# Two projections of a two-block transformer: one product over 512 columns in place of two over 256

## The chip, the cores and the metric

The kernel runs on one core of one Trainium2 chip. The metric is the device time of one execution in microseconds (us), the median of the runs shown. Five engines work beside each other and meet only at semaphores: PE (TensorE) multiplies matrices, PEld is its loading of weights, DVE (VectorE) and ACT (ScalarE) do the elementwise work, POOL (GpSimd) a few memsets, and SP (SyncE) issues the DMAs that bring the weights in.

## What is computed

256 tokens of width 2048 pass through two blocks in float32. The first block is an attention mixer followed by a feed-forward part, the second is another attention mixer with its own projections. What the change touches are the products of two large projections:

```python
def conv_geglu_ffn(h, w_up, conv_w, conv_b, w_down):
    u = h @ w_up                                   # 2048 -> 2 * 5632
    up = jnp.pad(u, ((0, 0), (1, 1), (0, 0)))
    u = conv_b + sum(up[:, t:t + S] * conv_w[t] for t in range(3))
    gate, val = jnp.split(u, 2, axis=-1)
    return (jax.nn.gelu(gate, approximate=True) * val) @ w_down
...
h = _rmsnorm(x, norm_g[l])                         # second block
proj = h @ w_in[l]
(qa, kca, vca, ksa, vsa, kwa, vwa, za, ga, qb, kb, vb, zb) = jnp.split(proj, offsets, axis=-1)
```

## The kernel before

**Number format.** TensorE multiplies a reduced float32 format here, so every float32 operand is held as a sum of two such numbers, a high and a low part. A product x·w is taken as high·high + high·low + low·high. An activation tile `h` (or `g`) is 128 x 512: columns 0 to 255 are the high parts of the 256 tokens, columns 256 to 511 their low parts. A weight tile of 128 x 128 exists as `hi` and as `lo`.

**A unit of product.** `mm3` (lines 326 to 332) handles one weight tile with three matmuls of 256 columns into the same 256 columns of a PSUM bank: `hi` by the high half (L329), `hi` by the low half (L330), `lo` by the high half (L331). `job_t` makes 128-column output tiles of these: for two output tiles at a time (`per=2`) it runs through the 16 weight tiles of one, then of the other, so that a pair takes 32 units. Both tiles of the pair share one PSUM bank of 512 float32 columns, 256 each. When the last unit is in, it queues the eviction `evac(i, ps)`. 3712 units in the program go through `mm3`.

**Weight stream.** All weights come in pieces of 128 x 1024 float32 (eight weight tiles) through 12 buffers `raw`. Per chunk of four weight tiles ACT makes `hi` (L290, a cast) and DVE makes `lo` (L291, raw minus hi), into six buffers of each; `execute` keeps four chunks ahead of the unit at hand. A `raw` buffer is fetched anew as soon as its last reader is done.

**Evictions.** In the feed-forward part `up` gives each pair (one gate tile, one value tile) to `glu`, which reads the bank directly: for each half an ACT activation (L1208, centre tap and bias) and two DVE operations (L1209, L1211, the side taps), then the gelu, a product (L1216) and the split into high and low parts (L503, L504). In the second block `tiles` hands the bank to a rotary embedding (`rope`) or to a gate (`ev_z`), which read it directly too. Between the units of the feed-forward part, every 20 of them, a batch of another product is woven in that runs on DVE alone (`ada_dve`, L456, straight from `raw`).

**Order.** The program is written as a list of units with side work that is advanced once every four units (`tick`); a scheduler then puts each engine's instructions into a fixed order. An engine executes its own list in that order and waits where an operand isn't there. Stages in time: up-projection of tiles 4 to 21 (about 545 to 752 us), half of the down-projection (to 879), up-projection of tiles 22 to 43 (to 1132), the other half (to 1286), second input projection and its attention heads (about 1300 to 1620), output projection.

Of the kernel before, what the change touches and what calls it, by code (L numbers as in the profile page):

```python
# [22 lines left out]
T = 256  # L23
D = 2048
KT = 16
EPS = 1e-6
NEG = -1e30
DFF = 5632
# [106 lines left out]
class Body:  # L135
# [8 lines left out]
        self.uid = 0  # L144
        self.active, self.waiting, self.now, self.last = [], [], 0, -99

    # ------------------------------------------------------------ tiles
    def nm(self, s):
        self.uid += 1
        return f"{s}_{self.uid}"  # L150
# [27 lines left out]
        o, w = CST[n]  # L178
        return self.ct[:, o + a:o + (w if b is None else b)]

    # ------------------------------------------------------------ cooperative side work
    def spawn(self, gen, group="", paced=False):
        (self.waiting if paced else self.active).append([gen, group, 0])

# [35 lines left out]
            v = get()  # L220
        return v

    # ------------------------------------------------------------ weight stream
    def flatten(self, prog):
        self.flat, self.plan, self.chunks = [], [], []
        self.uses = {}
        run = -1
        for u in prog:
            if u.kind == "c":
                self.flat.append(("c", u.fn, 0, 0, 0))  # L230
                continue
            if u.kind == "p":
                while len(self.plan) % PB:
                    self.plan.append(self.plan[-1])
                continue
            left, off = u.n, 0
            while left:
                pos = len(self.plan)
                room = PB - pos % PB
                n = min(left, room) if u.split else left  # L240
                assert n <= room
                for i in range(n):
                    self.plan.append((u.mat, u.kt, u.c0 + 128 * (off + i)))
                p = pos // PB
                if u.kind == "w":
                    c = self.chunks[-1] if self.chunks else None
                    if c is None or c[1] != pos or pos % PB == 0 or pos + n - c[0] > self.CHUNK:
                        self.chunks.append([pos, pos])
                        self.uses[p] = self.uses.get(p, 0) + 1
                    self.chunks[-1][1] = pos + n  # L250
                    fn = (lambda a, f=u.fn, o=off: f(a, o)) if u.split else u.fn
                    self.flat.append(("w", fn, pos, n, len(self.chunks) - 1))
                else:
                    self.uses[p] = self.uses.get(p, 0) + 1
                    self.flat.append(("r", (lambda a, f=u.fn, o=off: f(a, o)) if u.split else u.fn, pos, n, 0))
                left -= n
                off += n
        assert len(self.plan) <= NP * PB
        self.raw, self.hl = {}, {}
        self.nraw = self.nconv = 0  # L260
        self.free = self.NRAW
        self.npieces = (len(self.plan) + PB - 1) // PB
# [53 lines left out]
                since = 0  # L316
                self.tick()

    # ------------------------------------------------------------ products
    def align(self):  # L320
        return [U("p", 0, None, 0, 0, None)]

# [3 lines left out]
    def mm3(self, o, wt, x, first, last):  # L326
        hi, lo = wt
        mm = self.nc.tensor.matmul
        i = mm(o, hi, x[:, :T], start=first, stop=False)  # L329
        mm(o, hi, x[:, T:], start=False, stop=False)  # L330
        mm(o, lo, x[:, :T], start=False, stop=last)  # L331
        return i

    def job_t(self, mat, cols, kts, x, evac, per=2):
        out = []
# [161 lines left out]
        yield  # L497
        nc.vector.tensor_add(self.mod[:, col:col + 4], ps[:, :4], self.vec("ada_b", col, col + 4))

    # ------------------------------------------------------------ small parts  # L500
    def split(self, dst, src):
        n = src.shape[-1]
        self.nc.scalar.copy(dst[:, :n], src)  # L503
        self.nc.vector.tensor_sub(dst[:, n:2 * n], src, dst[:, :n].bitcast(F32))  # L504
# [113 lines left out]
        self.nc.scalar.activation(s, s if src is None else src, AF.Exp, bias=nm[:, j:j + 1], scale=scale,  # L618
                                  accum_out=sm[:, j:j + 1])

    # ------------------------------------------------------------ whole program
    def run(self, stop=None):
        with ExitStack() as es:
            pool = lambda **k: es.enter_context(self.tc.tile_pool(**k))
# [13 lines left out]
            self.execute()  # L638
            self.drain()

    # ------------------------------------------------------------ set-up
    def setup(self):
        nc = self.nc
        V, S = nc.vector, nc.scalar
# [149 lines left out]
        r = self.rsqrt(self.sxx, 2, 1.0 / D)  # L794
        yield from self.bcast(r, self.rbx)

    # ------------------------------------------------------------ first projection
    GROUPS = ((0, 2), (2, 2), (4, 4), (8, 4), (12, 4))

    def h_gen(self, g):  # L800
# [104 lines left out]
                self.pair = (self.s(4), self.w(), [])  # L905
            self.spawn(self.diff_head(h, *self.pair), "diff", True)

    # ------------------------------------------------------------ attention of the first block
    def diff_head(self, h, ss, keep, fin):
        nc = self.nc  # L910
        V, S, mm = nc.vector, nc.scalar, nc.tensor.matmul
# [172 lines left out]
                                                in1=self.vec("ffn_pre", a, b), op0=ALU.add, op1=ALU.mult)  # L1084
            self.nal = b

    # ------------------------------------------------------------ residual and norms between the parts
    def y_job(self, mat, kts, x, ko, ev):
        cols = [128 * i for i in range(16)]
        out = self.job_ko(mat, cols[:ko], kts, x, ev) if ko else []  # L1090
        return out + self.job_t(mat, cols[ko:], kts, x, lambda i, ps: ev(ko + i, ps))
# [102 lines left out]
            V.tensor_tensor(out=x_, in0=x_, in1=z_, op=ALU.add)  # L1194
            V.tensor_tensor(out=z_, in0=x_, in1=q_, op=ALU.mult)

    # ------------------------------------------------------------ feed-forward
    def p_ffn(self):
        nc = self.nc
        V, S = nc.vector, nc.scalar  # L1200
        g = {}
        cw = lambda t, ch: self.vec("conv_w", 88 * t + ch, 88 * t + ch + 1)

        def glu(i, us):
            t = self.w()
            for s, ch in ((0, i), (1, 44 + i)):
                u, o = us[s], t[:, s * T:s * T + T]
                S.activation(o, u, AF.Identity, bias=self.vec("conv_b", ch, ch + 1), scale=cw(1, ch))  # L1208
                V.scalar_tensor_tensor(out=o[:, 1:], in0=u[:, :T - 1], scalar=cw(0, ch), in1=o[:, 1:],  # L1209
                                       op0=ALU.mult, op1=ALU.add)  # L1210
                V.scalar_tensor_tensor(out=o[:, :T - 1], in0=u[:, 1:], scalar=cw(2, ch), in1=o[:, :T - 1],  # L1211
                                       op0=ALU.mult, op1=ALU.add)
            yield
            S.activation(t[:, :T], t[:, :T], AF.Gelu_apprx_tanh)
            yield
            V.tensor_tensor(out=t[:, :T], in0=t[:, :T], in1=t[:, T:], op=ALU.mult)  # L1216
            g[i] = d = self.g(F32R)
            self.split(d, t[:, :T])

        hx = lambda k: self.hs[k]  # L1220
        def before(kt):
            if kt % 2 == 0:
                self.need(lambda: True if self.nal > kt else None)
                self.make_h(kt // 2, self.al, self.mod[:, 48:64])
                self.tap("x1", self.x[kt // 2], kt // 2)

        def up(a, b):
            out = []
            for i in range(a, b):
                out += self.job_t("w_up", [128 * i, DFF + 128 * i], range(KT), hx,  # L1230
                                  lambda _, ps, i=i: self.spawn(glu(i, [ps[:, :T], ps[:, T:]]), "glu"))
            return out

        def end_a():
            self.accy = None

        prog = self.job_ko("w_up", sum([[128 * i, DFF + 128 * i] for i in range(KO)], []), range(KT), hx,
                           lambda i, ps: self.spawn(glu(i // 2, [ps[:, :T], ps[:, T:]]), "glu"), before)
        if LATE < 4:
            prog = _weave(prog, self.ada_pe([(p, 4 * LATE) for p in (3, 4)], 4, lambda: self.set_al(4 * LATE, 16)), 16)  # L1240
        prog += self.call(end_a)
        gx = lambda k: self.need(lambda: g.get(k))
        prog += _weave(up(KO, 22) + self.y_first("w_down", range(22), gx) + up(22, 44),
                       sum([self.ada_dve(5, 4 * c) for c in range(4)], []), 20)
        prog += self.call(lambda: self.drain("ada"))
        prog += self.y_second("w_down", range(22, 44), gx, 5, "ffn_post")

        def end():
            self.drain()
            g.clear()  # L1250
            self.post()
        return prog + self.call(end)

    # ------------------------------------------------------------ second block
    def p_block2(self):
        nc = self.nc
        V, S, mm = nc.vector, nc.scalar, nc.tensor.matmul
        full, w512 = slice(0, P), slice(0, 512)
        E = self.E = {}
        hx = lambda k: self.hs[k]  # L1260
        ks = range(KT)
# [32 lines left out]
                ev_rope("qa", "A")(i - 8, ps)  # L1294

        def tiles(n0, n, ev, per=2):
            return self.job_t("w_in2", [128 * (n0 + i) for i in range(n)], ks, hx, ev, per)

        def ev_v(t, ps):
            E["vsw"][t] = d = self.g()  # L1300
# [46 lines left out]
        m = self.job_n("w_in2", 8 * 128, 4, ks, hx, ev_v)  # L1347
        m += self.job_n("w_in2", 12 * 128, 2, ks, hx, ev_b)
        m += tiles(14, 1, ev_kb, 1)
        qa = tiles(15, 8, ev_rope("qa", "A"))  # L1350
        qb = tiles(23, 8, ev_rope("qb", "B"))
# [383 lines left out]
```

## Time and profile before

| what | value |
|---|---|
| median of 3 runs | 1745.68 us (1744.99 to 1745.84) |
| span of the profiled execution, first to last instruction | 1742.0 us |
| PE busy | 1702.2 us, 98% of the span, 13752 matmuls |
| weight loads (PEld) busy | 1562.2 us, 90% |
| DVE busy | 1181.3 us, 68% |
| ACT busy | 912.0 us, 52% |
| DMA queues, HBM read | 373.06 MB, 215 GB/s over the span |

The profile gives no separate time for the profiled execution itself; its span is 3.7 us below the median, and that remainder is taken to lie around the span, unchanged. Busy times count an instruction from its start to its modelled end. Matmuls overlap each other in the pipeline, so PE can read 100% busy at any pace: how fast it goes is seen from the distance of the starts, not from the mean duration.

### The profile page before, as it was taken

How to read it: one execution, taken by the hardware profiler on the slowest of the kernel's cores; microseconds unless marked ns; L12 is line 12 of the kernel's file. 1: busy time of each engine (PE TensorE's matmuls, PEld its weight loads, DVE VectorE, ACT ScalarE, POOL GpSimd, SP SyncE). 2: the span in 40 equal slices, each digit the busy share in tenths (PEclk: the TensorE clock that was granted, in tenths of full speed). 3: DMA queues.
4: the chain of work that ended last, by engine and by line, in shares of the span. 5: the costliest groups of instructions: out<-in, count | busy, mean ns of one | idle time of the engine just before them, and what ended most of it. 6: DMA issues, size and time to landing. Idle time of an engine off the chain costs nothing.

```text
span 1742.0 us, 35211 instructions
## 1 busy us (share of the span) xinstructions
PE 1702.2 (98%) x13752; PEld 1562.2 (90%) x13752; DVE 1181.3 (68%) x2363; ACT 912.0 (52%) x1866; POOL 8.9 (1%) x25
## 2 busy tenths in 40 slices
PE   6999999999989999999999999999989999999997
PEld 4778877788779999999999999999989899999996
DVE  7666688776578877765567766655576766767654
ACT  4444458554566655554455555555544445545553
POOL 0000000000000000000000000000000000000000
PEclk8999999999989999999999999999989999999998
DMA  9878874879845666666666655544445763333331
GB/s 382 331 287 301 306 298 174 299 300 379 342 142 201 223 220 211 206 233 222 218 217 219 218 183 184 186 175 170 169 145 188 255 243 109 135 140 138 137 131 49
DMA packets 104997, 377.43 MB, mean 217 GB/s; under 512 B 11776, under 2 KB 12032, under 8 KB 104832
## 3 DMA queue, kind: packets, MB, share of 16 engines
q1 hardware_dynamic: 103968, 373.51, 60.1%
q8 instruction: 107, 1.75, 0.4%
q10 hardware_dynamic: 864, 1.69, 0.3%
q14 instruction: 58, 0.48, 0.1%
HBM read 373.06 MB, written 2.10 MB: 215 GB/s over the span
## 4 chain that ended last, share of the span: by engine, by line
PE 96%; DVE 2%; ACT 0%; DMA 0%; issue 0%; ACTq 0%; DVEq 0%
PE ps L329 26%; PE ps L330 26%; PE ps L331 26%; PE ps L413 4%; PE ps L390 2%; PE ps L391 1%; PE ps L392 1%; PE ps L615 1%; PE ps L1137 1%; PE ps L1604 1%; PE ps L921 1%; PE ps L1625 1%; PE ps L1554 1%; PE ps L738 1%; DVE g L721 0%; PE ps L1442 0%
## 5 line engine op out<-in xcount | busy, mean ns | idle before, releaser
L329 PE MATMUL ps<-g,hi 128*128 128x256 f32 x3712 | 1067.3, 288 | 4.0 <-ACT g L1180 2.1
L330 PE MATMUL ps<-g,hi 128*128 128x256 f32 x3712 | 1053.1, 284 | 0.0
L331 PE MATMUL ps<-g,lo 128*128 128x256 f32 x3712 | 1051.8, 284 | 0.0
L290 ACT CAST hi<-raw 128x512 fp32r<-128x512 f32 x989 | 606.3, 619 | 615.1 <-PE ps L330 512.0
L291 DVE TENSOR_TENSOR lo<-raw,hi 128x512 fp32r<-128x512 f32 x989 | 670.5, 687 | 326.6 <-ACT hi L290 319.7
L329 PEld LDWEIGHTS ps<-g,hi 128*128 128x128 f32 x3712 | 713.1, 192 | 48.1 <-issue 18.8
L330 PEld LDWEIGHTS ps<-g,hi 128*128 128x128 f32 x3712 | 714.1, 192 | 5.7 <-issue 4.3
L331 PEld LDWEIGHTS ps<-g,lo 128*128 128x128 f32 x3712 | 713.4, 192 | 2.9 <-issue 2.1
L456 DVE SCALAR_TENSOR_TENSOR w<-raw,csil,w 128x512 f32<-128x512 f32 x105 | 78.6, 749 | 60.4 <-DMA raw<-wstream 59.8
L413 PE MATMUL ps<-raw,cz 128*32 128x512 f32 (+1 forms) x608 | 80.2, 566 | 0.0
L853 DVE TENSOR_TENSOR g<-g,ps 128x512 f32<-128x512 f32 (+1 forms) x48 | 31.7, 662 | 43.7 <-PE ps L331 43.7
L1208 ACT ACTIVATE w<-ps,vt 128x256 f32<-128x256 f32 x88 | 49.5, 562 | 18.9 <-DVE w L1211 18.6
L390 PE MATMUL ps<-hi,g 128*128 128x512 f32 (+1 forms) x136 | 51.9, 381 | 1.1 <-ACT g L814 1.1
L391 PE MATMUL ps<-lo,g 128*128 128x512 f32 (+1 forms) x136 | 50.0, 368 | 0.0
L392 PE MATMUL ps<-hi,g 128*128 128x512 f32 (+1 forms) x136 | 49.7, 366 | 0.0
L618 ACT ACTIVATE w<-ps,t 128x256 f32<-128x256 f32 (+1 forms) x80 | 33.5, 429 | 21.0 <-DVE t L1000 15.5
L503 ACT CAST g<-w 128x256 fp32r<-128x256 f32 x66 | 26.7, 406 | 33.7 <-DVE w L1216 17.1
L1211 DVE SCALAR_TENSOR_TENSOR w<-ps,vt,w 128x255 f32<-128x255 f32 x88 | 42.3, 481 | 2.3
L1209 DVE SCALAR_TENSOR_TENSOR w<-ps,vt,w 128x255 f32<-128x255 f32 x88 | 42.1, 479 | 1.2
L390 PEld LDWEIGHTS ps<-hi,g 128*128 128x128 f32 x136 | 25.6, 188 | 13.9 <-issue 4.6
L413 PEld LDWEIGHTS ps<-raw,cz 128*32 128x32 f32 x608 | 15.1, 111 | 18.0 <-issue 10.1
L504 DVE TENSOR_TENSOR g<-w,g 128x256 fp32r<-128x256 f32 x66 | 27.6, 419 | 4.2 <-ACT g L503 3.8
(254 smaller groups left out, 1072.5 us busy)
## 6 DMA issues: line engine op xcount, KB each, us to landing
raw<-wstream SPq DMA_DIRECT2D x704, 512.0 KB, 4.2
g<-xt SPq DMA_DIRECT2D x8, 256.0 KB, 5.7
out<-g SPq DMA_DIRECT2D x8, 256.0 KB, 2.4
g<-ropes ACTq DMA_DIRECT2D x2, 256.0 KB, 2.8
vt<-vecs ACTq DMA_DIRECT2D x1, 459.5 KB, 4.2
ct<-cst ACTq DMA_DIRECT2D x1, 265.0 KB, 3.1
g<-w ACTq DMA_DIRECT2D x1, 256.0 KB, 3.2
g<-pos SPq DMA_DIRECT2D x1, 160.0 KB, 3.8
```

Of the source, the lines that this page charges most:

```text
L290: self.nc.scalar.copy(hi[:, :n], src)
L291: self.nc.vector.tensor_sub(lo[:, :n], src, hi[:, :n].bitcast(F32))
L329: i = mm(o, hi, x[:, :T], start=first, stop=False)
L330: mm(o, hi, x[:, T:], start=False, stop=False)
L331: mm(o, lo, x[:, :T], start=False, stop=last)
L390: mm(ps[t][:, c], xh, hi, start=f and o == 0, stop=False)
L391: mm(ps[t][:, c], xh, lo, start=False, stop=False)
L392: mm(ps[t][:, c], xl, hi, start=False, stop=l and c.stop == w)
L413: mm(box["ps"][32 * q:32 * q + 32, o * 128:e], self.cz[:, a:a + 32], wt, start=first, stop=last and kt >= 12 and e == n * 128, tile_positi ...
L456: V.scalar_tensor_tensor(out=a, in0=w, scalar=c, in1=a, op0=ALU.mult, op1=ALU.add)
L1208: S.activation(o, u, AF.Identity, bias=self.vec("conv_b", ch, ch + 1), scale=cw(1, ch))
L1211: V.scalar_tensor_tensor(out=o[:, :T - 1], in0=u[:, 1:], scalar=cw(2, ch), in1=o[:, :T - 1], op0=ALU.mult, op1=ALU.add)
```

## The change

`job_t` is replaced by a new `job_w` in two places: in `up` (all up-projection pairs from tile 4 on) and in `tiles` (output tiles of the second input projection). A unit is now two matmuls in place of three: `hi` by the whole 512 columns of the activation tile into a whole PSUM bank, then `lo` by the 256 high columns into the upper half of that bank. Each output tile of a pair therefore has a bank of its own. The two halves of a bank are summed afterwards by `merge`: ACT copies the upper half to SBUF, DVE adds the lower half to it. What read the bank before now reads that SBUF tile.

```diff
+    def mmw(self, ps, wt, x, first, last):
+        hi, lo = wt
+        mm = self.nc.tensor.matmul
+        mm(ps, hi, x, start=first, stop=False)
+        mm(ps[:, T:], lo, x[:, :T], start=False, stop=last)
+
+    def merge(self, pss, out=None):
+        u = self.w() if out is None else out
+        for s, ps in enumerate(pss):
+            a = u[:, s * T:s * T + T]
+            self.nc.scalar.copy(a, ps[:, T:])
+            self.nc.vector.tensor_add(a, a, ps[:, :T])
+        return u
+
+    def job_w(self, mat, cols, kts, x, evac, per=2):
...
+                        if n == 0:
+                            pss.append(self.ps())
+                        self.mmw(pss[s], wt, x(kt), n == 0, n == len(kts) - 1)
+                        if s == len(cs) - 1 and n == len(kts) - 1:
+                            self.later(lambda: evac(i, pss))
...
@@ p_ffn, up
-                out += self.job_t("w_up", [128 * i, DFF + 128 * i], range(KT), hx,
-                                  lambda _, ps, i=i: self.spawn(glu(i, [ps[:, :T], ps[:, T:]]), "glu"))
+                out += self.job_w("w_up", [128 * i, DFF + 128 * i], range(KT), hx,
+                                  lambda _, pss, i=i: self.spawn(glu_w(i, pss), "glu"))
...
+        def glu_w(i, pss):
+            u = self.merge(pss)
+            yield from glu(i, [u[:, :T], u[:, T:]])
@@ p_block2, tiles
-            return self.job_t("w_in2", [128 * (n0 + i) for i in range(n)], ks, hx, ev, per)
+            return self.job_w("w_in2", [128 * (n0 + i) for i in range(n)], ks, hx, lambda i, pss: ev(i, self.merge(pss)), per)
```

How this stands on the engines is shown at two places. First PE, inside the up-projection: three consecutive units before (`ps` is the bank, `g` the activation tile, `hi` and `lo` the weights):

```order
L329 MATMUL ps_8699<-g_6511,hi_8658 128x256
L330 MATMUL ps_8699<-g_6511,hi_8658 128x256
L331 MATMUL ps_8699<-g_6511,lo_8659 128x256
L329 MATMUL ps_8699<-g_6515,hi_8658 128x256
L330 MATMUL ps_8699<-g_6515,hi_8658 128x256
L331 MATMUL ps_8699<-g_6515,lo_8659 128x256
L329 MATMUL ps_8699<-g_6590,hi_8658 128x256
L330 MATMUL ps_8699<-g_6590,hi_8658 128x256
L331 MATMUL ps_8699<-g_6590,lo_8659 128x256
```

The nine matmuls load weights nine times, `hi` twice in a row for each unit. Now PE at such a place, three units of the changed kernel:

```order
L337 MATMUL ps_9086<-g_6511,hi_9046 128x512
L338 MATMUL ps_9086<-g_6511,lo_9047 128x256
L337 MATMUL ps_9086<-g_6515,hi_9046 128x512
L338 MATMUL ps_9086<-g_6515,lo_9047 128x256
L337 MATMUL ps_9086<-g_6590,hi_9046 128x512
L338 MATMUL ps_9086<-g_6590,lo_9047 128x256
```

Six matmuls and six loads stand for the nine; apart from this the order of PE's work is almost that of before. There are 1744 rows of L337 in the changed kernel, 1280 of the up-projection and 464 of the second block.

Second place, DVE at the eviction of the last pair before the down-projection (`w_9623` collects the pair's convolution, `ps_9460` is its bank, `g_9666` the result), before:

```order
L291 TENSOR_TENSOR lo_9634<-raw_9255,hi_9633 128x512
L1209 SCALAR_TENSOR_TENSOR w_9623<-ps_9460,vt,w_9623 128x255
L1211 SCALAR_TENSOR_TENSOR w_9623<-ps_9460,vt,w_9623 128x255
L291 TENSOR_TENSOR lo_9653<-raw_9305,hi_9652 128x512
L1209 SCALAR_TENSOR_TENSOR w_9623<-ps_9460,vt,w_9623 128x255
L1211 SCALAR_TENSOR_TENSOR w_9623<-ps_9460,vt,w_9623 128x255
L291 TENSOR_TENSOR lo_9673<-raw_9344,hi_9672 128x512
L1216 TENSOR_TENSOR w_9623<-w_9623 128x256
L291 TENSOR_TENSOR lo_9689<-raw_9344,hi_9688 128x512
L504 TENSOR_TENSOR g_9666<-w_9623,g_9666 128x256
```

DVE on the same pair in the changed kernel (`ps_9013` and `ps_9086` are the two banks, `w_9150` the merged tile, `g_9198` the result):

```order
L345 TENSOR_TENSOR w_9150<-w_9150,ps_9013 128x256
L291 TENSOR_TENSOR lo_9108<-raw_8840,hi_9107 128x512
L1240 SCALAR_TENSOR_TENSOR w_9155<-w_9150,vt,w_9155 128x255
L1242 SCALAR_TENSOR_TENSOR w_9155<-w_9150,vt,w_9155 128x255
L291 TENSOR_TENSOR lo_9120<-raw_8840,hi_9119 128x512
L291 TENSOR_TENSOR lo_9134<-raw_8846,hi_9133 128x512
L291 TENSOR_TENSOR lo_9166<-raw_8846,hi_9165 128x512
L345 TENSOR_TENSOR w_9150<-w_9150,ps_9086 128x256
L291 TENSOR_TENSOR lo_9185<-raw_8884,hi_9184 128x512
L1240 SCALAR_TENSOR_TENSOR w_9155<-w_9150,vt,w_9155 128x255
L1242 SCALAR_TENSOR_TENSOR w_9155<-w_9150,vt,w_9155 128x255
```

Two additions (L345) have come in. The first bank's half is now merged and convolved three conversions earlier than the second's, because its bank is complete when half the pair is; before, both halves came together at the end of the pair.

## Rows read from the trace of the kernel before

**Rows 1.** The page: the span; busy time, share of the span and instructions of each engine.

```profile
span 1742.0 us, 35211 instructions
...
PE 1702.2 (98%) x13752; PEld 1562.2 (90%) x13752; DVE 1181.3 (68%) x2363; ACT 912.0 (52%) x1866; POOL 8.9 (1%) x25
```

**Rows 2.** The page: shares of the chain that ended last, by engine.

```profile
PE 96%; DVE 2%; ACT 0%; DMA 0%; issue 0%; ACTq 0%; DVEq 0%
```

**Rows 3.** PE's groups by line and shape: count, busy us, mean ns, idle before.

```profile
L329 PE MATMUL ps<-g,hi 128*128 128x256 f32 x3712 | 1067.3, 288 | 4.0 <-ACT g L1180 2.1 <-ACT g L1175 2.0
...
L390 PE MATMUL ps<-hi,g 128*128 128x512 f32 x104 | 42.5, 408 | 1.1 <-ACT g L814 1.1
```

**Rows 4.** Stretches: us, busy of PE, PEld, DVE, ACT, POOL (count); granted clock, DMA share, GB/s.

```profile
545.00:752.00 207.00, 207.00 (x1728) 207.00 (x1728) 161.03 (x299) 119.74 (x226) 0.00 (x0) 1.00 0.63 214
...
879.00:1005.00 126.00, 126.00 (x1053) 126.00 (x1052) 92.09 (x164) 70.02 (x128) 0.00 (x0) 1.00 0.65 218
1005.00:1132.00 127.00, 127.00 (x1061) 127.00 (x1060) 86.71 (x156) 71.44 (x132) 0.00 (x0) 1.00 0.53 184
1395.00:1620.00 225.00, 225.00 (x1757) 211.42 (x1754) 152.35 (x385) 113.73 (x291) 0.93 (x3) 1.00 0.43 151
```

**Rows 5.** PE in order of time, up-projection: start us, duration us, line, tiles, shape.

```profile
900.04 0.28 PE L330 MATMUL ps<-g,hi 128*128 128x256 f32 x1
900.16 0.28 PE L331 MATMUL ps<-g,lo 128*128 128x256 f32 x1
```

**Rows 6.** PE in order of time, a product of 512-column matmuls, from its first on.

```profile
1353.36 0.40 PE L390 MATMUL ps<-hi,g 128*128 128x512 f32 x1
1353.59 0.40 PE L391 MATMUL ps<-lo,g 128*128 128x512 f32 x1
1353.83 0.39 PE L392 MATMUL ps<-hi,g 128*128 128x512 f32 x1
...
1354.74 0.39 PE L390 MATMUL ps<-hi,g 128*128 128x512 f32 x1
...
1359.96 0.39 PE L392 MATMUL ps<-hi,g 128*128 128x512 f32 x1
```

**Rows 7.** PE in order of time where 512-column matmuls end and 256-column ones begin.

```profile
64.18 0.39 PE L392 MATMUL ps<-hi,g 128*128 128x512 f32 x1
64.41 0.28 PE L329 MATMUL ps<-g,hi 128*128 128x256 f32 x1
64.52 0.28 PE L330 MATMUL ps<-g,hi 128*128 128x256 f32 x1
```

**Rows 8.** Groups by line and shape, ACT and DVE: operations like the added ones.

```profile
L1597 ACT COPY w<-ps 128x256 f32<-128x256 f32 x16 | 6.2, 386 | 0.0
...
L1195 DVE TENSOR_TENSOR g<-g,ps 128x256 f32<-128x256 f32 x4 | 1.7, 418 | 0.1
```

**Rows 9.** Waits in 545 to 752 us: who waited for whom, us, times, longest.

```profile
ACT hi L290 <- PE ps L330: 59.4, 86, 1.2
DVE w L456 <- DMA raw<-wstream: 23.6, 16, 3.8
DVE lo L291 <- ACT hi L290: 17.9, 31, 0.8
```

**Rows 10.** Waits in 879 to 1005 us, the same.

```profile
ACT hi L290 <- PE ps L330: 46.4, 66, 1.2
DVE lo L291 <- ACT hi L290: 21.6, 34, 0.8
DVE w L456 <- DMA raw<-wstream: 9.9, 10, 2.0
```

**Rows 11.** PE in order of time in a stretch at the lower clock.

```profile
497.97 0.41 PE L329 MATMUL ps<-g,hi 128*128 128x256 f32 x1
498.18 0.41 PE L330 MATMUL ps<-g,hi 128*128 128x256 f32 x1
```

More of the change, by code (lines that the diff above doesn't have):

```diff
@@ L332, in mm3, with fn @@
         return i
+    def mmw(self, ps, wt, x, first, last):
[11 more added lines that the diff above has]
+    def job_w(self, mat, cols, kts, x, evac, per=2):
+        out = []
+        kts = list(kts)
+        for i in range(0, len(cols), per):
+            cs = cols[i:i + per]
+            pss = []
+            for s, c0 in enumerate(cs):
+                for n, kt in enumerate(kts):
+                    def fn(wt, s=s, n=n, kt=kt, pss=pss, i=i, cs=cs):
+                        if n == 0:
[3 more added lines that the diff above has]
+                            self.later(lambda: evac(i, pss))
+                    out.append(U("w", 1, mat, kt, c0, fn))
+        return out
     def job_t(self, mat, cols, kts, x, evac, per=2):
```

## The prediction

> **What bounds the kernel now.** I read the page's first two lines and the chain of waits first. PE is busy for 98% of the span [rows 1], and of the chain that ended last 96% is PE's own work [rows 2]: hardly anything makes PE wait for long, so the time is what PE needs to pass its matmuls through. DVE at 68% and ACT at 52% [rows 1] have room on average.
>
> What a matmul costs can't be read from its mean duration. The groups give 288 ns for 256 columns and 408 ns for 512 [rows 3], but these overlap in the pipeline. The price is the distance between starts. In order of time, the 256-column matmuls of the up-projection start 0.12 us apart [rows 5]. The stretches give a finer figure: 1728 matmuls in 207 us, 1053 in 126, 1061 in 127 [rows 4], which is 0.1198, 0.1197 and 0.1197 us. Counts and spacing agree, so there are no holes in these stretches, and I take 0.1197 us. The granted clock there is 1.00, the 2.4 GHz level [rows 4], at which 256 columns stream in 256 / 2.4 = 106.7 ns. So about 13 ns are paid beyond the columns.
>
> Is that per column or per instruction? The 512-column matmuls answer. From 1354.74 to 1359.96 us there are 23 distances [rows 6]: 5.22 / 23 = 0.2270 us. 512 columns stream in 213.3 ns, so again some 13 ns are left over. The surplus is paid per instruction and not per column. At the lower clock it isn't seen: 256 columns take 0.21 us there [rows 11], which is 256 / 1.2 and nothing more. The four stretches in which nearly all of the changed units lie run at 1.00 [rows 4], so the surplus is there to be saved.
>
> **The change, part by part.**
>
> *PE, the unit.* Before: three matmuls of 256 columns, 3 x 0.1197 = 0.3591 us. After: one of 512 and one of 256, 0.2270 + 0.1197 = 0.3467 us. The columns are the same, 768; one instruction with its load of weights goes, and with it 0.0124 us. The changed kernel has 1744 such units: 1744 x 0.0124 = 21.6 us. All of it lies on the chain, since PE is dense there.
>
> The uncertain point is that no stream of before alternates 512 and 256. The nearest rows are those around a switch. After a run of 256 columns the first two 512-column matmuls are followed after 0.23 and 0.24 us [rows 6], somewhat more than the settled 0.2270. Where 512 gives way to 256, the distances are 0.23 and then 0.11 us [rows 7], somewhat less. So the dear end is 0.235 + 0.1197 = 0.3547 us per unit, a gain of 0.0044 x 1744 = 7.7 us; the cheap end is 0.23 + 0.11 = 0.34, a gain of 0.0191 x 1744 = 33.3 us. In the new stream each 512 both follows and precedes a 256, so the two effects meet in every unit and work against each other; I take the settled paces, which lie between.
>
> The Trainium skill has a rule that speaks against a gain of this size: "TensorE: Matmul & The Clock Gate", section "Back-to-back issue gap", gives N / 2.4 plus 2.5 ns for a warm matmul of N columns. By it one instruction fewer saves 2.5 ns per unit, 4.4 us in all. The rows above show 13 ns in its place, at both widths, so the trace disagrees and the trace is used.
>
> *PE, the rest.* 3712 - 1744 = 1968 units keep three matmuls. The order of the rest of PE's work is nearly unchanged. No price.
>
> *ACT and DVE, the merge.* Per half bank one ACT copy of 128 x 256 from PSUM, 386 ns by the nearest row, and one DVE addition of that shape with a PSUM operand, 418 ns [rows 8]. There are 80 halves in the up-projection and 29 in the second block, 109 in all: 42 us of ACT and 46 us of DVE. The later steps of the eviction read SBUF where they read PSUM; I price that at nought, as the wait of PE for any of them has a cover of several conversions. All of the 88 us must hide under PE, and the place where this is tightest is the up-projection with the woven product on DVE.
>
> In 545 to 752 us DVE is busy for 161.0 of 207 us [rows 4]. 18 pairs, 36 additions, bring 15.0 us: 176.0. The stretch itself shrinks by 18 x 32 x 0.0124 = 7.1 us to 199.9. That leaves 23.9 us idle. Two kinds of waits fill the idle time today: 23.6 us for a DMA into `raw` ahead of L456, and 17.9 us for ACT's `hi` [rows 9]. The second kind is slack, because ACT itself waits for PE to release a `hi` buffer, 59.4 us [rows 9]: both conversions stand as far ahead of PE as six buffers let them. The first kind is no slack while DVE runs ahead, but it shrinks as DVE comes later to the same data. With the DMA waits whole the account is 176.0 + 23.6 = 199.6 of 199.9 us: it just closes. In 879 to 1005 us it is 92.1 + 22 x 0.418 + 9.9 = 111.2 of 121.6 us [rows 4, 10]. In the second block, 1395 to 1620 us, 152.4 + 28 x 0.418 = 164.1 of about 220 [rows 4]. ACT in the first stretch goes from 119.7 by 36 x 0.386 to 133.6 of 199.9. So I take nought for stalls. If the cover fails, PE waits for `hi` or `lo`, and what is late next is everything, for PE is the chain. The bound from below is also nought: no row shows PE waiting in these stretches, so a shorter hold of a bank can't give anything back.
>
> *The wait that is added.* ACT's convolution step now waits for DVE's addition, which waits for ACT's copy. Queued behind it on ACT are the casts to `hi` of the following chunks; PE waits for these. One such hand-over is shorter than the lead of a chunk of four units, 4 x 0.3467 = 1.39 us, and the lead is several chunks. The first half's merge stands ahead of the end of the pair in the new order, so the last pair ahead of the down-projection has only one half left to merge when it ends. No price.
>
> *DMA.* The weights are the same, in the same pieces; they are asked for 3.5% faster in these stretches, where the DMA share is 0.43 to 0.65 [rows 4]. No price.
>
> Sum against the profiled execution: span 1742.0 - 21.6 = 1720.4 us. The median of the runs is 3.7 us above that span, and I leave this remainder: 1745.7 - 21.6 = **1724.1 us**, a gain of 1.2%.
>
> **The rivals.**
>
> *A, alternation is dear.* Each 512-column matmul pays its price after a switch, 0.235 us, because in the new stream it always stands behind a 256. For it: both first distances [rows 6]. Against it: in the other direction the switch is cheap [rows 7]. Time: 1745.7 - 7.7 = 1738.0.
>
> *B, nothing is saved.* The surplus of the instruction that goes comes back in the 512-column one, because in the alternating stream it pays the dearer of the two distances after a switch, 0.24 us [rows 6]: 0.24 + 0.1197 = 0.3597 against 0.3591 us per unit, 1745.7 + 1744 x 0.0006 = 1746.7. For it: that one distance. Against it: it has settled to 0.2270 a few matmuls later. The rule of the skill's page named above comes out near this, at 1745.7 - 4.4 = 1741.3, for a reason of its own.
>
> *C, alternation is cheap.* Each 512 gives way to a 256 and pays 0.34 per unit [rows 7]: 1712.4.
>
> *D, the cover on DVE is partly gone.* Half of the waits in E come out on PE: 1724.1 + 14.4 = 1738.5.
>
> *E, slower: DVE becomes the bound in the two woven stretches.* If all its present waits stay whole, because each hand-over of the merge makes new ones where old ones shrink, the first stretch needs 176.0 + 23.6 + 17.9 = 217.5 us against 199.9, the second 101.3 + 9.9 + 21.6 = 132.8 against 121.6 [rows 4, 9, 10]. That is 17.6 + 11.2 = 28.8 us of stalls, more than the 21.6 saved: 1752.9. It turns the sign as soon as three quarters of the 28.8 come out. For it: DVE would be at 88% there. Against it: 17.9 and 21.6 of it are waits at a full lead, which DVE loses first when it falls behind.
>
> That the change doesn't do what it says can be left out: the order shows 512-column matmuls in place of pairs.
>
> **How the numbers follow.** Forecast, 1720 to 1728 with 1724.1 its centre: 0.64. A: 0.12, B: 0.03, C: 0.09, D: 0.07, E: 0.05. For 8 in 10 the range takes in A and D and reaches into C: 1714.0 to 1738.5; left out are B, E and part of C. About 0.2%, 3.5 us, is what a measurement of this kernel can tell from no change. Faster by more than that are the forecast, A, C and D, 0.92, less 0.01 for a D that goes far; slower is E, 0.05; between them lie B and that tail, 0.04.
>
> **What would show it.** Right: in the changed kernel's up-projection the starts alternate by about 0.23 and 0.12 us, a window there holds two matmuls per 0.347 us, and the groups of PE show no idle time ahead of L337 and L338. The idle time of DVE in the woven stretches goes down with its waits for ACT's `hi`, not with PE waiting. A or C: the same windows hold two matmuls per 0.355 or 0.34 us without idle PE. D or E: idle PE or its loads ahead of L337 and L338, released by `hi` L290 or `lo` L291, between 530 and 1000 us, and a granted clock below 1.00 there. What makes the prediction wrong in size is the distance of an alternating stream; what makes it wrong in sign is DVE.

## The result, and the profile after

The changed kernel takes **1729.47 us** (median of 4 runs, 1728.7 to 1730.86); the kernel before took 1745.76 beside it. The ratio is 0.991 with a 95% interval of 0.9898 to 0.9922. That is 16.3 us less where 21.6 were forecast: the direction holds, the time lies in the range of 1714.0 to 1738.5, and a quarter of the forecast gain is missing. It lies above the band from 1720 to 1728 that had a chance of 0.64, between the forecast and rival *A*.

The page of the changed kernel, the lines that answer to [rows 1] and [rows 2]: the span, the busy time of each engine, and the shares of the chain that ended last.

```profile
span 1727.3 us, 31993 instructions
...
PE 1687.2 (98%) x12008; PEld 1468.4 (85%) x12008; DVE 1215.4 (70%) x2472; ACT 948.5 (55%) x1975; POOL 8.9 (1%) x25
...
PE 96%; DVE 2%; DMA 1%; ACT 0%; issue 0%; ACTq 0%; DVEq 0%
```

PE has 1744 matmuls fewer (13752 to 12008), DVE and ACT 109 operations more each, and the chain is PE's as before. The profiled execution took 1729.1 us with this span of 1727.3; the span went down by 14.7 us.

The groups of the new lines: count, busy us, mean ns of one, then the idle time of the engine ahead of them.

```profile
L337 PE MATMUL ps<-g,hi 128*128 128x512 f32 x1744 | 619.0, 399 | 0.0
L338 PE MATMUL ps<-g,lo 128*128 128x256 f32 x1744 | 489.5, 281 | 0.0
...
L345 DVE TENSOR_TENSOR w<-w,ps 128x256 f32<-128x256 f32 x109 | 45.0, 415 | 0.8 <-ACT w L344 0.8
...
L344 ACT COPY w<-ps 128x256 f32<-128x256 f32 x109 | 40.1, 369 | 0.0
```

The 0.0 behind L337 and L338 is the first thing to read: PE never stood idle ahead of the new matmuls. So nothing that DVE or ACT does can have eaten the missing gain by making PE wait. The waits of the woven stretch, 545 to 752 us, say the same from the other side (who waited for whom: us in total, times, longest):

```profile
ACT hi L290 <- PE ps L337: 46.0, 83, 1.4
DVE lo L291 <- ACT hi L290: 21.1, 47, 1.0
...
DVE w L487 <- DMA raw<-wstream: 4.5, 7, 1.9
```

ACT still waits for PE to give back `hi` buffers, 46.0 us against 59.4 in [rows 9]. DVE's waits for a DMA fell from 23.6 to 4.5 us, so the additions of the merge found room. Its waits for ACT's `hi` did not shrink (17.9 to 21.1 us).

So the time must be in PE's own pace. In order of time, PE inside the first up-projection stretch (start us, duration us, line, tiles, shape):

```profile
599.66 0.40 PE L337 MATMUL ps<-g,hi 128*128 128x512 f32 x1
599.90 0.28 PE L338 MATMUL ps<-g,lo 128*128 128x256 f32 x1
600.01 0.40 PE L337 MATMUL ps<-g,hi 128*128 128x512 f32 x1
600.24 0.28 PE L338 MATMUL ps<-g,lo 128*128 128x256 f32 x1
600.36 0.40 PE L337 MATMUL ps<-g,hi 128*128 128x512 f32 x1
600.60 0.28 PE L338 MATMUL ps<-g,lo 128*128 128x256 f32 x1
600.72 0.40 PE L337 MATMUL ps<-g,hi 128*128 128x512 f32 x1
...
604.96 0.40 PE L337 MATMUL ps<-g,hi 128*128 128x512 f32 x1
```

From one L337 to the next it is 0.35, 0.35, 0.36 us, over and over; from 599.66 to 604.96 there are 15 units: 5.30 / 15 = **0.3533 us** a unit. The forecast was 0.3467. Now the same kernel, same instructions, later in the same projection:

```profile
1029.77 0.39 PE L337 MATMUL ps<-g,hi 128*128 128x512 f32 x1
1030.00 0.28 PE L338 MATMUL ps<-g,lo 128*128 128x256 f32 x1
1030.12 0.39 PE L337 MATMUL ps<-g,hi 128*128 128x512 f32 x1
1030.35 0.28 PE L338 MATMUL ps<-g,lo 128*128 128x256 f32 x1
1030.46 0.39 PE L337 MATMUL ps<-g,hi 128*128 128x512 f32 x1
...
1032.54 0.39 PE L337 MATMUL ps<-g,hi 128*128 128x512 f32 x1
```

Eight units in 2.77 us, **0.346** a unit; over this whole stretch it is 0.347 (352 units in some 122 us, the last line of the second table below): the forecast pace. The stream has two rhythms. Which one holds where is quickest to read from how many matmuls fall into a window of fixed length. PE alone, four stretches of the up-projection (us, PE busy with its count, granted clock, DMA share, GB/s):

```profile
560.00:650.00 90.00, 90.00 (x511) 1.00 0.71 229
665.00:740.00 75.00, 75.00 (x427) 1.00 0.70 229
900.00:990.00 90.00, 90.00 (x511) 1.00 0.71 223
1010.00:1100.00 90.00, 90.00 (x521) 1.00 0.58 192
```

Ninety microseconds hold 2 x 90 / 0.3533 = 509 matmuls in the one rhythm and 2 x 90 / 0.3467 = 519 in the other, and one or two are counted across the edges. The first three stretches are slow, the last is fast, and the granted clock is 1.00 in all of them. How many units that touches, again by windows, of L337 alone (PE busy with the count, PEld the same):

```profile
500.00:760.00 260.00, 203.69 (x576) 108.24 (x576) 1.00 0.66 214
...
860.00:1003.00 143.00, 124.56 (x353) 66.19 (x353) 1.00 0.70 221
1003.00:1130.00 127.00, 122.15 (x352) 65.78 (x352) 1.00 0.58 189
```

576 + 353 = 929 units of the up-projection (one of them counted twice at the edge) run in the slow rhythm: 929 x (0.3533 - 0.3467) = 6.1 us.

To set this against the forecast, the pace of before is needed more finely than the prediction had it. Between two folds of the woven product (a fold is eight matmuls of one column) the kernel before runs 320 units of three matmuls without a gap. The first and the last of their L329:

```profile
661.19 0.36 PE L329 MATMUL ps<-g,hi 128*128 128x256 f32 x1
...
776.10 0.28 PE L329 MATMUL ps<-g,hi 128*128 128x256 f32 x1
```

That is 114.91 / 319 = 0.3602 us a unit, not 0.3591: a window's count takes in the matmuls that straddle its edges, so 207 us over 1728 came out a little short. A unit thus saves 0.3602 - 0.3467 = 0.0135 us in the fast rhythm and 0.0069 in the slow one. Where the gain fell can be read from the first matmul after the up-projection and the down-projection, first in the kernel before, then in the changed one:

```profile
1281.70 0.58 PE L329 MATMUL ps<-g,hi 128*128 128x256 f32 x1 [1.97 <-ACT g L1175]
```

```profile
1270.54 0.80 PE L329 MATMUL ps<-g,hi 128*128 128x256 f32 x2 [1.97 <-ACT g L1206]
```

By then 11.2 us are won, with the 1280 units of the up-projection, for which 1280 x 0.0124 = 15.9 were forecast. Of the 14.7 us between the spans 3.5 are left for the 464 units of the second block, where 5.8 were forecast; they run in short pieces, partly in the one rhythm and partly in the other.

### The profile page after: what moved, and what is told of

It is laid out like the page before. It is cut to its first block, busy times and chain, and to the rows that moved or that the text cites. A ratio compares the mean times of both kernels' runs of the same rounds, so it can differ in the third digit from the quotient of the medians.

```text
span 1727.3 us, 31993 instructions
## 1 busy us (share of the span) xinstructions
PE 1687.2 (98%) x12008; PEld 1468.4 (85%) x12008; DVE 1215.4 (70%) x2472; ACT 948.5 (55%) x1975; POOL 8.9 (1%) x25
## 4 chain that ended last, share of the span: by engine, by line
PE 96%; DVE 2%; DMA 1%; ACT 0%; issue 0%; ACTq 0%; DVEq 0%
PE ps L337 24%; PE ps L329 14%; PE ps L330 14%; PE ps L331 14%; PE ps L338 12%; PE ps L444 4%; PE ps L421 2%; PE ps L422 1%; PE ps L423 1%; PE ps L646 1%; PE ps L1168 1%; PE ps L1639 1%; PE ps L952 1%; PE ps L1660 1%; PE ps L1589 1%; PE ps L769 1%
## 5 line engine op out<-in xcount | busy, mean ns | idle before, releaser
L337 PE MATMUL ps<-g,hi 128*128 128x512 f32 x1744 | 619.0, 399 | 0.0
L329 PE MATMUL ps<-g,hi 128*128 128x256 f32 x1968 | 569.2, 290 | 4.0 <-ACT g L1211 2.1
L330 PE MATMUL ps<-g,hi 128*128 128x256 f32 x1968 | 559.3, 284 | 0.0
L338 PE MATMUL ps<-g,lo 128*128 128x256 f32 x1744 | 489.5, 281 | 0.0
L329 PEld LDWEIGHTS ps<-g,hi 128*128 128x128 f32 x1968 | 378.3, 193 | 44.6 <-issue 18.0
L337 PEld LDWEIGHTS ps<-g,hi 128*128 128x128 f32 x1744 | 327.4, 188 | 80.4 <-issue 1.7
L330 PEld LDWEIGHTS ps<-g,hi 128*128 128x128 f32 x1968 | 379.2, 193 | 5.7 <-issue 4.3
L338 PEld LDWEIGHTS ps<-g,lo 128*128 128x128 f32 x1744 | 329.6, 189 | 0.0
L1239 ACT ACTIVATE w<-w,vt 128x256 f32<-128x256 f32 x80 | 47.7, 599 | 1.9 <-DVE w L345 1.6
L345 DVE TENSOR_TENSOR w<-w,ps 128x256 f32<-128x256 f32 x109 | 45.0, 415 | 0.8 <-ACT w L344 0.8
L344 ACT COPY w<-ps 128x256 f32<-128x256 f32 x109 | 40.1, 369 | 0.0
```

The source lines that it names most:

```text
L337: mm(ps, hi, x, start=first, stop=False)
L338: mm(ps[:, T:], lo, x[:, :T], start=False, stop=last)
```

## The experiments

**Theory.** The price is PE's own: an alternating stream of 512 and 256 columns has a distance per unit of its own, whatever the other engines do. **Rivals.** The merge, or DVE's traffic beside it, slows PE down without making it wait; or the price hangs on the place in the program.

### The merge alone

The products stay three matmuls of 256 columns, but into a whole bank, so that all of the merge is kept and nothing of the wide product.

```diff
-        mm(ps, hi, x, start=first, stop=False)
+        mm(ps[:, :T], hi, x[:, :T], start=first, stop=False)
+        mm(ps[:, T:], hi, x[:, T:], start=False, stop=False)
         mm(ps[:, T:], lo, x[:, :T], start=False, stop=last)
```

> Two banks per pair and the merge by ACT and DVE as in the changed kernel, but each unit with three matmuls of 256 columns as before. If the merge is hidden under PE (as the sum had it), the time is that of the kernel before, 1744 to 1748 us, and no PE idle time shows ahead of the units. If the 5 us that the change fell short of the sum are stalls from the merge, it is 1750 to 1753 us.

Measured: 1745.02 us against 1744.18 of the kernel before, ratio 1.0002 (0.9993 to 1.0011). The window from 560 to 650 us with all engines (PE, PEld, DVE, ACT, POOL), first of the kernel before, then of this one:

```profile
560.00:650.00 90.00, 90.00 (x752) 90.00 (x752) 71.20 (x132) 53.24 (x101) 0.00 (x0) 1.00 0.67 224
```

```profile
560.00:650.00 90.00, 90.00 (x752) 90.00 (x751) 76.98 (x151) 57.94 (x120) 0.00 (x0) 1.00 0.69 222
```

DVE carries 5.8 us more and ACT 4.7, and PE passes the same 752 matmuls. The merge costs nothing that the interval of about 0.1% could show, so the gain, and what is missing of it, belongs to the matmuls.

It also tells how far the additions explain the shorter DMA waits. From 545 to 752 us of this kernel:

```profile
DVE w L488 <- DMA raw<-wstream: 17.6, 13, 2.5
```

With the additions alone the waits fall from 23.6 to 17.6 us. The way from there to 4.5 came with the wide product; why, no run here shows.

### Without the merge, and without the woven work

Two kernels with the wide product, each without one neighbour: the first leaves out the sum of the halves in the up-projection, the second 15 of 16 of DVE's operations of the woven product.

```diff
 # no_sum
-            u = self.merge(pss)
-            yield from glu(i, [u[:, :T], u[:, T:]])
+            yield from glu(i, [pss[0][:, T:], pss[1][:, T:]])
 # no_axpy
-                self.axpy(box["acc"][:, o * 128:o * 128 + wt.shape[-1]], wt, kt)
+                if kt == 0:
+                    self.axpy(box["acc"][:, o * 128:o * 128 + wt.shape[-1]], wt, kt)
```

> The changed kernel without the merge in the up-projection: the convolution reads the upper half of each bank directly and the lower half (high weights by high activations) is left out of the result. DVE loses 80 additions (33 us), ACT 80 copies (30 us). If the merge costs PE time, the time falls below the changed kernel's 1729 by up to 5 us; if it is hidden, 1728 to 1731 us, and the starts in the up-projection keep the same distances.

> The changed kernel with 15 of 16 DVE operations of the woven product left out (its result is wrong there); the weights still stream in. In the changed kernel a unit takes 0.353 us up to 1003 us, where the woven part ends, and 0.347 us after it. If DVE's traffic makes the slow rhythm, every unit of the up-projection takes 0.347 us here: 960 units by 0.0066 us, some 6 us less, about 1723 us. If the rhythm is one of two that the alternating stream can lock into, whole stretches are still at 0.353, not tied to the end of the woven part, and the time is anything from 1722 to 1730 us.

Measured: 1730.69 and 1731.38 us, one run each, not below the changed kernel. Both hold 511 matmuls from 560 to 650 us and 521 from 1010 to 1100, as the changed kernel does. The second one's first window, with all engines:

```profile
560.00:650.00 90.00, 90.00 (x511) 78.08 (x510) 70.94 (x140) 60.55 (x121) 0.00 (x0) 1.00 0.71 230
```

The same window of the changed kernel:

```profile
560.00:650.00 90.00, 90.00 (x511) 78.03 (x510) 79.13 (x155) 60.29 (x122) 0.00 (x0) 1.00 0.71 229
```

DVE is at 70.94 us where it has 79.13 in the changed kernel, and the rhythm is the same. So neither the merge in the up-projection nor the woven operations on DVE set it. Both rivals about the neighbours fall. The transfers of the weights went on in both kernels, so these two runs say nothing of DMA; the kernels with a push, further below, do.

### Four wide ones, then four narrow ones

```diff
         mm(ps, hi, x, start=first, stop=False)
-        mm(ps[:, T:], lo, x[:, :T], start=False, stop=last)
+        self.held.append((ps, lo, x))
+        if len(self.held) == 4:
+            for k, (p, l, y) in enumerate(self.held):
+                mm(p[:, T:], l, y[:, :T], start=False, stop=last and k == 3)
+            self.held = []
```

> Same matmuls as the changed kernel, but per chunk of four units first the four of 512 columns, then the four of 256. If what was lost against the sum comes from alternating at every instruction, four units take near 4 x 0.2270 + 4 x 0.1197 = 1.387 us plus one pair of switches (some 0.01 to 0.02 us), or 0.350 a unit: 1723.5 to 1728 us. If the slower rhythm isn't bound to the alternation, it shows here too: 0.353 a unit, 1729 to 1731 us.

Measured: 1727.1 us (1726.29 to 1729.56), ratio 0.9905 (0.9888 to 0.9921). PE in order of time; rows of one kind are run together here, with their count at the end:

```profile
600.85 1.09 PE L338 MATMUL ps<-g,hi 128*128 128x512 f32 x4
601.78 0.63 PE L342 MATMUL ps<-g,lo 128*128 128x256 f32 x4
602.25 1.09 PE L338 MATMUL ps<-g,hi 128*128 128x512 f32 x4
...
655.58 1.09 PE L338 MATMUL ps<-g,hi 128*128 128x512 f32 x4
```

From 600.85 to 655.58 there are 39 groups of four units: 1.403 us a group, 0.351 a unit, between the slow rhythm and the settled paces. If the 0.0066 us by which the slow rhythm exceeds 0.3467 were paid per switch between widths, a quarter of the switches would leave a quarter, 0.0017; more than half, 0.004, is left. The windows show the one pace in all stretches (515 and 516 matmuls in 90 us); the time itself can't be told from the changed kernel's, for the intervals overlap.

### Every second unit the other way round

The stream becomes 512, 256, 256, 512, 512, 256 and so on: equal widths stand side by side.

```diff
+        a = lambda f, l: mm(ps, hi, x, start=f, stop=l)
+        b = lambda l: mm(ps[:, T:], lo, x[:, :T], start=False, stop=l)
+        self.turn = first or not self.turn
+        if self.turn:
+            a(first, False)
+            b(last)
+        else:
+            b(False)
+            a(False, last)
```

> The changed kernel with every second unit turned round, so that the stream runs 512, 256, 256, 512, 512, 256, and so on: half as many switches of width. If each switch costs, a unit comes to lie between the settled 0.3467 and the 0.3503 that groups of four gave, with a time of 1722 to 1727 us. If instead the single alternation is only unlucky in its rhythm, any value from 0.3467 to 0.3533 can come out, the same in all of a stretch.

Measured: 1724.37 us (1723.41 to 1725.64), ratio 0.9881 (0.9864 to 0.9897); the changed kernel's interval begins at 0.9898. PE in order of time, pairs run together:

```profile
600.01 0.63 PE L338 MATMUL ps<-g,hi 128*128 128x512 f32 x2
600.48 0.40 PE L339 MATMUL ps<-g,lo 128*128 128x256 f32 x2
...
602.10 0.63 PE L338 MATMUL ps<-g,hi 128*128 128x512 f32 x2
...
656.44 0.63 PE L338 MATMUL ps<-g,hi 128*128 128x512 f32 x2
```

Six units in 2.09 us, and 162 units from 600.01 to 656.44, 0.3483 a unit, and this in all stretches: 518, 520 and 518 matmuls in the three windows of 90 us. No two rhythms are seen in these windows. It doesn't reach 0.3467, but no stretch falls to 0.3533. With half of the switches a quarter of the surplus is left, 0.0016 us, less than the groups kept with a quarter of the switches. So it is not a price per switch.

### Only at the start of a tile

All units but the first of an output tile have the narrow matmul first, so two wide ones meet once in 16 units, at the tile's beginning.

```diff
+        if first:
+            mm(ps, hi, x, start=True, stop=False)
+            mm(ps[:, T:], lo, x[:, :T], start=False, stop=False)
+        else:
+            mm(ps[:, T:], lo, x[:, :T], start=False, stop=False)
+            mm(ps, hi, x, start=False, stop=last)
```

> The changed kernel with the two matmuls of a unit in the other order (256 columns, then 512), except in the first unit of an output tile, which must begin with the 512. The stream alternates as before, but meets two 512 and two 256 in a row at each tile's start, every 16 units. If the alternating stream can lock into either of two rhythms (0.3533 or 0.3467 us a unit) and a disturbance can change which, the tiles take one or the other, and where the stream is in which changes against the changed kernel: 1722 to 1731 us. If the slow rhythm comes from the place in the program, 544 to 1003 us stays at 0.3533 and the time at 1729.

Measured: 1731.14 us (one run), with 512, 511 and 513 matmuls in the three windows of 90 us. The stream falls back into the slow rhythm after each such place, in the late stretch too, which is fast in the changed kernel. In the second block it isn't always so: ten units from 1403.18 to 1406.64 us take 0.346 each. So one irregular place doesn't by itself lead to the fast rhythm; what would, this run doesn't tell.

### A push at the beginning

If the rhythm is something that the stream inherits, a change far ahead should move it where nothing else differs. In these two kernels the first 16 (or 18) units of the up-projection are turned as above; every later instruction of PE is that of the changed kernel.

```diff
+        self.units += 1
+        if self.units <= 16 and self.units % 2 == 0:      # 19 in the second kernel
+            mm(ps[:, T:], lo, x[:, :T], start=False, stop=False)
+            mm(ps, hi, x, start=False, stop=last)
+        else:
...
```

> The changed kernel with every second unit turned round in the first 16 units of the up-projection (545 to 550 us) alone; all later units alternate plainly. If the stream stays in the rhythm that it was left in until something disturbs it, the plain units from 551 to the gap near 660 us run wholly at 0.3533 or wholly at 0.3467, perhaps not the 0.3533 of the changed kernel: 1725 to 1731 us. If the rhythm belongs to the place, they are at 0.3533 as there.

> The same with the first 18 units, so that the plain alternation begins two units later. Same two expectations; if a rhythm once begun lasts, the two kernels may differ from 551 to 660 us by 0.0066 us a unit, some 2 us, though all of their matmuls there are the same.

Measured: 1727.74 and 1726.69 us, one run each. The windows of the first one, PE alone, to be held against the four of the changed kernel above:

```profile
560.00:650.00 90.00, 90.00 (x511) 1.00 0.71 231
665.00:740.00 75.00, 75.00 (x435) 1.00 0.70 231
```

Directly behind the push both kernels are in the slow rhythm, so the difference that was expected from 551 us on isn't there. But from 665 to 740 us there are 435 matmuls where the changed kernel has 427: that stretch has become fast (2 x 75 / 0.3467 = 433), in both kernels alike. What lies between is a fold of the woven product. In the changed kernel the same place reads:

```profile
657.84 0.28 PE L338 MATMUL ps<-g,lo 128*128 128x256 f32 x1
657.96 0.95 PE L526 MATMUL ps<-ct,w 128*128 128x1 f32 x8
658.77 0.48 PE L337 MATMUL ps<-g,hi 128*128 128x512 f32 x1
```

The changed kernel is slow on both sides of it; the pushed one is slow ahead of it and fast behind it. At a later fold, about 1002 us, the changed kernel itself goes from slow to fast. So the same instructions in the same place were seen in either rhythm, and the folds are where it was seen to change. The load on DMA doesn't set it: the fast window above has a DMA share of 0.70 and 231 GB/s, as much as the slow one of the changed kernel.

That the push did it is likely, not shown. In four kernels with plain alternation and no push (the changed one, the two without a neighbour, and the one of the next section) the window from 665 to 740 us holds 426 or 427 matmuls, in both pushed kernels 435. But each kernel has one trace, the pushed ones ran on another chip than the other experiments with plain alternation, and whether the rhythm also differs from one execution of a kernel to the next was not tested. What it is in TensorE that keeps the rhythm isn't shown by any of these runs.

### The wide product in more places

The same product also in the down-projection, in the rest of the first output projection and in the last one: 1088 units more, 2832 in all. The evictions there add the two halves into the sum that they already keep.

```diff
-        return out + self.job_t(mat, cols[ko:], kts, x, lambda i, ps: ev(ko + i, ps))
+        return out + self.job_w(mat, cols[ko:], kts, x, lambda i, ps: ev(ko + i, ps))
...
+            V.tensor_add(a, a, ps[h][:, T:])
+            V.tensor_add(a, a, ps[h][:, :T])
...
-        wo = lambda kts, ev: self.job_t("w_out", ...
+        wo = lambda kts, ev: self.job_w("w_out", ...
```

> The changed kernel, with the same product also in the down-projection, the rest of the first output projection and the last one: 1088 units more (704, 128, 256). At 0.3533 to 0.3467 in place of 0.3591 us each they save 6.3 to 13.5 us if the additional evictions (two additions per half with a PSUM operand in place of one over the pair) are hidden: 1716 to 1723 us. If the end of the program, where the evictions are not under other PE work, pays for them, up to 3 us of this is given back.

Measured: 1722.33 us, ratio 0.9859 (0.9841 to 0.9877). Its four stretches of wide units between the folds, of L337 alone (PE busy with the count, PEld the same); the third is for the most part the down-projection, now wide too:

```profile
545.00:660.50 115.50, 113.11 (x320) 60.13 (x320) 1.00 0.68 223
660.90:774.50 113.60, 113.19 (x320) 60.13 (x320) 1.00 0.69 222
774.90:886.40 111.50, 111.07 (x320) 59.84 (x320) 1.00 0.71 227
886.80:1000.40 113.60, 113.19 (x320) 60.13 (x320) 1.00 0.68 223
```

The third is fast between slow ones, and from 1010 to 1100 us the stream is fast again (521 matmuls). It changes from slow to fast to slow to fast, each time at a fold; the fast rhythm doesn't belong to the late part of the program alone.

Three of the runs lie at 1722.3 to 1722.4 us and one at 1715.87. The trace is that of a run at 1722.3. An estimate from it: with its 3 x 320 slow units fast, it would take 960 x 0.0066 = 6.3 us less, 1716.0. So the quick run is what a change of rhythm between executions of one kernel would look like; it has no trace, and this stays open.

Both edits together:

> Every second unit turned round, and the wide product in the down-projection and both output projections too: 2832 units at 0.3483 us in place of 0.3591, a gain of 30.6 us if evictions stay hidden: 1714.5 us against 1745.1. If the evictions at the end show, up to 3 us more; if the turned order settles at 0.3533 elsewhere, 1722.

Measured: **1714.41 us** (1713.43 to 1716.27), ratio 0.9825 (0.9809 to 0.9842), the best of all. Its new group, to be read as those above:

```profile
L338 PE MATMUL ps<-g,hi 128*128 128x512 f32 x2832 | 909.6, 398 | 0.0
```

No idle time ahead of PE here either, with 2832 units. Against the turned kernel the 1088 further units bring 1724.4 - 1714.4 = 10.0 us, 9.2 ns each, where 0.3602 - 0.3483 makes 11.9.

## Why the prediction was right, and where it was off

**What bounds the kernel:** right. PE was the chain before and after, and the gain came from PE alone; the merge by itself changed nothing that could be measured (1.0002, 0.9993 to 1.0011).

**PE, the unit:** the mechanism was right, and its size was the term that was off. The step put 0.2270 + 0.1197 = 0.3467 us for a unit of the alternating stream. Measured: 0.347 in one rhythm, 0.3533 in the other, with most of the up-projection in the second. By the prediction's own signs the early stretches look like *A* (0.355) and only the late one like the forecast. Averaged over all 1744 units the gain is 16.3 / 1744 = 9.3 ns in place of 12.4. The text named this as the uncertain point and saw that no row of before alternates the widths; it then took the settled paces on the thought that a dear and a cheap switch cancel. In the slow rhythm they don't: the distances behind L337 there are 0.23 to 0.24 us, and those behind L338 0.11 to 0.12. The cheap switch was read out of rounding: starts are printed to 0.01 us, and 0.23 + 0.11 can't be told from 0.2270 + 0.1197. The price of before was a little low too, 0.3591 for 0.3602, which made the forecast gain 1.1 ns a unit smaller and hid part of the miss. Rows of separate streams could not have told that there are two rhythms. How near the median came to 1724.1 depended on which rhythm held where, and that was not foreseen: as an estimate, 1744 units all fast would have made about 1722 us, all slow about 1734.

**The rule of the Trainium skill**, "TensorE: Matmul & The Clock Gate", section "Back-to-back issue gap", made 4.4 us of the saved instructions, an estimate. The section gives that rule for the gap of a matmul by itself and says that in a stream of loads and matmuls both set the spacing, so it was no fair rival here. The 16.3 us measured disagree with it; the 13 ns per instruction from [rows 4] and [rows 6] were nearer, as a price for equal widths.

**The merge:** right. Its operations took 369 ns on ACT and 415 on DVE, where 386 and 418 were put, and their 85 us of busy time hid under PE. The argument that the DMA waits shrink as DVE comes later was borne out in part: 23.6 to 17.6 us with the merge alone, 4.5 in the changed kernel, where PE's pace differs too. The sign that the text gave, fewer waits of DVE for ACT's `hi`, did not come (17.9 to 21.1).

**The added wait:** right. ACT's convolution waited 1.6 us in all for the addition, and PE shows no idle time ahead of the new lines.

**The remainder around the span:** the 3.7 us were taken as lying around it. The profiled execution of after has 1.8 there, and so has that of the merge alone, whose span equals that of before (1743.81 and 1742.0). If before had the same, its profiled execution was 1.9 us quicker than its median. That did no harm, since the sum only subtracts, but it would be most of why the medians differ by 16.3 and the spans by 14.7.

**The rivals.** *A* is half right: its 0.3547 a unit, with 0.235 us behind each 512, is near the slow rhythm's 0.3533, but it was to hold everywhere and hold for a 512 behind any 256; the fast rhythm, and the turned order, in which every second 512 still stands behind a 256 and the unit takes 0.3483, go against it. *B* falls: both rhythms gain on 0.3602. *C*, 0.34 a unit, was seen nowhere. *D* and *E* fall with the 0.0 of idle time ahead of L337 and L338.

## What to carry to other kernels

Price a matmul by the distance of the starts in the stream in which it will stand: a stream that mixed widths here had paces that neither width showed alone, and counting matmuls in windows of equal length found them in one look. For the pace itself, take two starts far apart with no gap between them: a window's count has matmuls on both edges. Merging two matmuls of 256 columns with the same weights saved 7 to 13 ns a unit here; turning every second unit, so that equal widths meet, made it some 12 in every stretch looked at, for no operation more. The work added on DVE and ACT cost nothing here, where both had waits to give up, and the idle time ahead of the bound engine's new lines says whether that is so.

## What had not been expected of the hardware

One and the same sequence, 512 and 256 columns in turn with a load of weights each, ran at 0.3533 us a unit (three units in 0.35, 0.35 and 0.36) or at 0.347, both at a granted clock of 1.00, each for a hundred microseconds and more without a change. Which one it was stayed the same without the merge and without nearly all of the woven work on DVE, and differed in two kernels in which the order of 16 or 18 units some 100 us earlier had been changed. Changes between the two rhythms in the up-projection were seen only where other small matmuls stood between. Turned units took 0.3483, groups of four 0.351. The cause in TensorE stays open.
